# A two-block language model layer on one core: the RWKV inverse kept in both triangular forms, new lengths and grouped pieces in the scheduler, three more slots

## The chip, the core and the metric

The kernel runs on one core of one Trainium2 chip. The metric is the device time of one launch in microseconds (us). Shown are the median of three runs and the profile of one execution.

## What is computed

256 tokens with 1024 features go through two transformer blocks. The first block projects the normed stream into three branches: an RWKV-7 recurrence (8 heads of 64), stick-breaking attention (8 heads of 64), and attention over a memory of 256 rows (4 heads of 128). The branches are gated, merged, projected and added, and a convolutional feed-forward layer follows. The second block has ALiBi attention beside an HGRN-2 recurrence, then a PEER layer (for each token and head 16 of 16384 experts), and a final norm. The part that the change touches most is the recurrence of RWKV-7:

```python
def step(S, inp):
    r_t, w_t, k_t, v_t, kk_t, a_t = inp
    sa = jnp.einsum('bhij,bhj->bhi', S, -kk_t)
    S = (S * w_t[:, :, None, :]
         + sa[..., None] * (kk_t * a_t)[:, :, None, :]
         + v_t[..., None] * k_t[:, :, None, :])
    y_t = jnp.einsum('bhij,bhj->bhi', S, r_t)
    return S, y_t
```

The kernel computes it in chunks of 64 tokens. Within a chunk each head needs the inverse of I + A, where A is strictly lower triangular, 64 x 64; there are 8 heads and 4 chunks, so 32 such inverses.

## The kernel before

**Recording and scheduling.** The kernel's methods don't issue instructions; they record them. Each recorded operation has an engine, a modelled length, and the tiles that it reads and writes. Consecutive products on TensorE that write the same bank are recorded as one piece (`Program.op`, lines 244 to 281) while the piece's modelled length stays under 0.7 us; between two banks that are written in turn this is allowed too where a flag, `join`, is set. `Program.run` (lines 304 to 440) then lays out an order for each engine by list scheduling: of the operations whose inputs are ready by the model and whose tiles have a free slot, the one that can start first, and among those that can start at the same time the one with the longest remaining path. It also models TensorE's clock, and when that is low it prefers operations that fill the array. `emit` (line 442) issues everything from one line, 456, so every instruction of the trace carries L456 (or L450, for table loads); tiles tell the instructions apart. The order on an engine is fixed at build time; on the chip, semaphores between engines decide when each instruction starts.

**The two programs.** Everything up to the PEER layer's start (block 1, block 2, the first PEER queries) is laid out as one program (line 1757), the PEER layer and the final norm as a second one (line 1765, `serial=True`). In the second, operations other than weight products go first on TensorE.

**Weight products.** All large products are computed in three fp32r passes (hi x hi, hi x lo, lo x hi), so each weight tile is loaded by DMA (tile `wraw`), rounded by ScalarE (`whi`) and subtracted by VectorE (`wlo`). Their PSUM banks are tile `psg` (three banks); everything smaller uses tile `ps` (five banks). In one form 256 columns stream per product, in the other 512; `mm` (line 502) models the length.

**Slots.** Working tiles of 1024 words take one of 25 slots (`NSLOT`, line 1782) from their first use to their last. Groups of work (rwkv, stick, mem, gates, main) have reserves of slots and of PSUM banks (line 1784).

**RWKV and its inverse.** `rwkv` starts at line 777. Token-major forms and the Gram matrices (`at`, `bt`, `ct`, `et`) come first, with 64 x 64 products, two chunks side by side in the array. The inverse (lines 927 to 963) is built by doubling, from blocks of 2 to blocks of 64. `tu` holds the upper form (transposed inverse), `tl` the lower one; both are kept for two token blocks (`tb`) of 8 heads and 2 chunks each. At each of four levels `pairs` (line 896) multiplies `at` and `tl`, VectorE masks the result into `y`, `pairs` multiplies `y` and `tu`, VectorE subtracts that from `tu`, and `lower(tb)` (line 931) transposes `tu` into `tl`. A last level has blocks of 32.

```python
        for b in LEVELS[:-1]:
            mb = bcm(self.cst(f"m{b}"), 8)
            for tb in range(2):
                self.mul(y[:, tb], pairs(self.ps(), at, tl, tb), mb)
            for tb in range(2):
                self.sub(tu[:, tb], tu[:, tb], pairs(self.ps(), y, tu, tb))
                lower(tb)
```

[...] 

Behind the inverse come W, the chunk's map G (`g_done`, line 983), the states and the outputs, a group norm, and the split into `yh` and `yl`. The gates' loop then uses the branches in the order stick, memory, RWKV.

Of the kernel before, what the change touches and what calls it, by code (L numbers as in the profile page):

```python
# [19 lines left out]
P = 128  # L20
T = 256
# [65 lines left out]
# ---------------------------------------------------------------------------  # L87
# Tiles and instructions are first recorded; an order of issue is then laid
# out by list scheduling (longest remaining path first) and handed to Tile,
# which places the semaphores.  # L90
# [5 lines left out]
# activation functions outside every table set, the time of a switch  # L96
TABLE = {AF.Exp: "e", AF.Ln: "e", AF.Sigmoid: "s", AF.Tanh: "s", AF.Sqrt: "q", AF.Silu: "w", AF.Gelu: "g"}
SWITCH = 1.28
WINDOW = 3.4133

# [37 lines left out]
class Buf:  # L138
    """A tile: it holds one of its tag's slots from its first use to its last."""
# [68 lines left out]
class Op:  # L208
    __slots__ = ("eng", "calls", "cost", "deps", "succ", "bufs", "first", "level", "ndep", "ready", "idx", "table", "start", "area", "gemm", "bonus", "prio")


class Program:
    def __init__(self, tc):
        self.tc, self.nc = tc, tc.nc
        self.ops, self.tags, self.pools = [], {}, {}
        self.group = None
        self.reserve = {}
        self.count = 0
        self.free_at = {e: 0.0 for e in ("PE", "ACT", "DVE", "POOL", "SP")}
        self.dma_free = 0.0  # L220
        self.bonus = 0.0
        # tiles that the next instruction takes along, to have them before it holds others
        self.also = ()
        self.merge = True
        self.table = None
        self.win, self.work, self.cold = 0.0, 0.0, True
        self.join = False

# [15 lines left out]
    def op(self, eng, method, args, kw, reads, writes, cost, area=1.0, hold=(), gemm=False):  # L244
        call = (eng, method, args, kw)
        last = self.ops[-1] if self.ops else None
        if (eng == "PE" and self.merge and last is not None and last.eng == "PE" and last.cost + cost < 0.7 and last.area == area
# [4 lines left out]
        else:  # L252
            o = Op()
            o.eng, o.calls, o.cost, o.deps, o.bufs, o.idx = eng, [call], cost, {}, {}, len(self.ops)
            o.gemm, o.bonus = gemm, self.bonus
# [27 lines left out]
    # ------------------------------------------------------------ scheduling  # L283
    # the tensor engine's clock is halved for a window of 3.41 us if the array
    # did little work in the window before
# [6 lines left out]
    def clock(self, s, o):  # L292
# [9 lines left out]
        return t - s  # L302

    def run(self, reserve=None, serial=False):
# [53 lines left out]
        while left:  # L358
            best = None
            for e in engines:  # L360
# [3 lines left out]
                if e == "PE":  # L364
                    self.window(f)
                    keep = self.cold or self.work < KEEP * (f - self.win)
                for o in ready[e]:
# [39 lines left out]
            else:  # L407
# [3 lines left out]
                if o.eng == "PE":  # L411
                    end = s + self.clock(s, o)
                free_at[o.eng] = end
            order.append((s, len(order), o))
# [44 lines left out]
class Kernel:  # L459
# [9 lines left out]
    # ---------------------------------------------------------------- helpers  # L469
# [32 lines left out]
    def mm(self, out, lhsT, rhs, start=True, stop=True, skip=False, hold=None, after=None):  # L502
        n = rhs.n
        if rhs.dt == F32:
            cost = max(n / 600, lhsT.shape[1] / 640) + 0.005
        elif rhs.dt == F32R:
            cost = n / 2400 + 0.0025
        else:
            cost = n / 2400 + 0.0025
# [3 lines left out]
        elif area == 0.25:  # L513
            cost = 0.029 + 0.00084 * n
        elif rhs.dt == F32:
            area *= n / 600 / cost
# [3 lines left out]
        self.pr.op("PE", "matmul", (out, lhsT, rhs), kw, [lhsT, rhs, after], [out], cost, area, hold or (), rhs.dt == F32R)  # L520

    # in_ [k, m] -> out [m, k]
    def tr(self, out, in_):
        self.pr.op("PE", "transpose", (out, in_, self.cst("ident")), {}, [in_], [out], 0.11, TR_AREA)

    # the same for 64 x 64 of half rr of the partitions, in place (a transpose's output starts at partition 0)
    def tr64(self, out, in_, rr):
        if rr.start:
            self.mm(out, in_, self.cst("ident")[rr, rr])
            return  # L530
        self.pr.op("PE", "transpose", (out, in_, self.cst("ident")[rr, rr]), {}, [in_], [out], 0.0425, TR_AREA / 4)
# [49 lines left out]
    # after: not before this has been computed  # L581
# [13 lines left out]
    # a weight tile of n columns, loaded at once, as parts of up to 1024 columns  # L595
# [28 lines left out]
    # out^T tiles: [128 features, 256 tokens] in pairs, one PSUM bank per pair;  # L624
    # weight tiles are [128 k, 2 features blocks, kt, 128]
    # early: the first tiles, whose last products wait for the last two k-tiles
# [23 lines left out]
    # natural: [128 tokens, 512 features] for both token blocks; weight tiles are [128 k, 4 kt, 512]  # L650
# [16 lines left out]
    # 1 / sqrt(mean of squares + eps) per token, on every partition  # L667
# [26 lines left out]
    # (x * g) * rstd, split  # L694
# [7 lines left out]
    # x * g, split; the products are to be scaled by rstd, which is returned  # L702
# [7 lines left out]
    # rstd with tokens on partitions  # L710
# [8 lines left out]
    # both features of a bank by rstd  # L719
# [23 lines left out]
    # sums over each head's 64 features of [128 (2 heads), 4, 256] -> [128 t, (tb, 8 heads)]  # L743
# [8 lines left out]
    # [128 t, (tb, 8 heads)] repeated over each head's 64 features  # L752
# [6 lines left out]
    # -> PSUM [128 (2 heads x 64), 256 t] for pair p  # L759
# [4 lines left out]
    # ---------------------------------------------------------------- block 1: RWKV  # L764
# [12 lines left out]
    def rwkv(self, R, K, V, L):  # L777
# [7 lines left out]
        # decay, learning rate  # L785
# [12 lines left out]
        # kk, normalised per head  # L798
# [16 lines left out]
        # k' = k (1 + (a - 1) k_a), b = kk a  # L815
# [4 lines left out]
        # decays within chunks of 64  # L820
# [10 lines left out]
        # kappa = kk P_{t-1}, rho = r P_t, b / P, k' / P; the bonus times v  # L831
        # (kappa and rho side by side, two pairs of heads per tile)
# [10 lines left out]
        # scaled to the chunk's end  # L843
# [10 lines left out]
        # token-major forms: [128 t, (tb, 8 heads, 64)]  # L854
        NB, NE_, NV = self.get("nb"), self.get("ne"), self.get("nv")
        # (kappa and B V side by side, a tile per token block)
# [12 lines left out]
        # Gram matrices per head and chunk, stacked over the two chunks of a token block  # L869
# [22 lines left out]
        # products with v: B V, V^T E^T, and the state's increment from k'  # L892
        YT, H = self.get("yt"), self.get("h")

        # per head and chunk: left^T right, the two chunks of a block side by side in the array
# [11 lines left out]
        # banks by chunk parity u; f(p, tb, u, par, rows of the chunk, out)  # L907
# [19 lines left out]
        # (I + A)^-1 by doubling  # L927
# [3 lines left out]
        def lower(tb):  # L931
            ps = self.ps()
            for h in range(8):
                for rr in half:
                    self.tr64(ps[rr, h * 64:h * 64 + 64], tu[rr, tb, h, :], rr)
            act(tl[:, tb], ps.rearrange("p (h d) -> p h d", h=8))

        for tb in range(2):
            self.mul(tu[:, tb], at[:, tb], bcm(self.cst("m1"), 8))
            self.sub(tu[:, tb], id8, tu[:, tb])  # L940
            lower(tb)
        for b in LEVELS[:-1]:
# [3 lines left out]
            for tb in range(2):  # L946
                self.sub(tu[:, tb], tu[:, tb], pairs(self.ps(), y, tu, tb))
                lower(tb)
        # the last level: one block of 32 below the diagonal
# [19 lines left out]
        # W = -T [kappa | B V]  # L969
# [9 lines left out]
        # per chunk: the state's map G^T, its increment H, and Z in place of rho  # L979
# [3 lines left out]
        def g_done(u, b, ps):  # L983
            g = q422(G)[:, :, b, u, :]
            tb = b.start
            self.mul(g[:, :, 0, :], bcm(self.cst("id2"), 4), peu[:, :, tb, u, :].to_broadcast([P, 4, 64]))
            self.add(g, g, ps)
# [14 lines left out]
        # states S_1 = H_0, S_{c+1} = G_c S_c + H_c, in place of H (slot c holds S_{c+1})  # L1002
# [12 lines left out]
        # outputs y^T  # L1015
# [12 lines left out]
        # group norm per head, gains, bonus, gate  # L1028
# [35 lines left out]
    # ---------------------------------------------------------------- block 1: stick breaking  # L1064
# [5 lines left out]
    # 1 / rms of each head's features, [128 t, (tb, heads)], of [128 t, (tb, 512)]  # L1070
# [13 lines left out]
    # [128 t, (tb, 512)] -> PSUM [128 features, (2 of the blocks, 256 t)], block pair pp  # L1084
# [62 lines left out]
    # ---------------------------------------------------------------- block 1: memory  # L1147
# [44 lines left out]
    # ---------------------------------------------------------------- block 1  # L1192
# [6 lines left out]
    def block1(self):  # L1199
# [12 lines left out]
        pr.group = "stick"  # L1212
        rs = self.rstd_n(rb)
        S = self.big(3, "sb")
        for n, x in enumerate(S):
            self.gemm_n("w_sb", (n * 2, n * 2 + 1), hh, hl, self.evac_n(lambda tb: x[:, tb * 512:(tb + 1) * 512], rs))
        self.stick(*S)
        pr.group = "mem"
        ME = self.big(2, "mem")
        self.load_x(ME, "memT", H[0])  # L1220
        MH = self.big(4, "mh", F32R)
        mh, ml = self.ktiles(MH[:2]), self.ktiles(MH[2:])
        rm = self.norm_late(ME, "mem_norm_g", mh, ml, RE[1])
        MK, MV = self.big(2, "mkv")
        rsm = self.rstd_n(rm)
        for n, x in enumerate((MK, MV)):
            self.gemm_n("w_mem", (n * 2, n * 2 + 1), mh, ml, self.evac_n(lambda tb: x[:, tb * 512:(tb + 1) * 512], rsm))
        pr.group = "mem"
        MQ = self.get("mq")
        self.gemm_n("w_memq", range(2), hh, hl, self.evac_n(lambda tb: MQ[:, tb * 512:(tb + 1) * 512], rs))  # L1230
        self.memory(MQ, MK, MV)
# [636 lines left out]
```

## Time and profile before

| what | value |
| --- | --- |
| device time, median of 3 runs | 1618.37 us (1616.47 to 1623.98) |
| span of the profiled execution | 1608.7 us |
| TensorE (PE) busy | 1569.9 us, 98% |
| VectorE (DVE) busy | 1158.2 us, 72% |
| ScalarE (ACT) busy | 763.9 us, 47% |
| GpSimd (POOL) busy | 124.9 us, 8% |
| mean granted TensorE clock | 0.984 |
| DMA | 249.13 MB, mean 155 GB/s |

The span is counted from the first to the last instruction. Of the profiled execution the page gives the span alone; the runs' median is 9.7 us above it. Engine times are unions of instruction times; matmuls are pipelined and their ends are modelled, so a busy TensorE may still be waiting inside a train of small products. The granted clock is 1.00 at full speed (2.4 GHz) and 0.5 at the lower level (1.2 GHz).

### The profile page before, as it was taken

The numbers are of one execution on the slowest core, as the hardware profiler recorded it, in microseconds if no ns is written. First come the engines' busy times: TensorE is split into PE (matmuls) and PEld (weight loads), VectorE is DVE, ScalarE is ACT, GpSimd is POOL, SyncE is SP. The second block draws the span as 40 slices with busy tenths as digits, with TensorE's granted clock in tenths as the row PEclk, the third lists the DMA queues.
The fourth block names the chain that finished last, engine by engine and source line by source line (L and its number), as shares of the span: only waits on it lengthen the run. The fifth ranks groups of instructions, "written<-read, shape, count | busy, mean of one in ns | idle before, by whom it ended". The sixth has DMA issues, their size and how long they took to land.

```text
span 1608.7 us, 29184 instructions
## 1 busy us (share of the span) xinstructions
PE 1569.9 (98%) x12260; PEld 1422.0 (88%) x12260; DVE 1158.2 (72%) x1970; ACT 763.9 (47%) x1026; POOL 124.9 (8%) x112
## 2 busy tenths in 40 slices
PE   6999999999999999899999999999999999999998
PEld 5976778999999999779999999999998888888886
DVE  8872246666898866977878789888867888555554
ACT  4642246544576645365544445433344333444444
POOL 5010000002321112402000000000000000000000
PEclk9988799999999999999999999999999999999999
DMA  6420122255555545233554455434344444555553
GB/s 220 157 79 27 53 80 80 100 186 187 184 184 184 181 169 223 79 139 125 184 184 174 172 183 184 180 132 158 133 167 172 147 156 157 183 183 189 200 188 131
DMA packets 38436, 249.13 MB, mean 155 GB/s; under 512 B 4000, under 2 KB 7456, under 8 KB 9504
## 3 DMA queue, kind: packets, MB, share of 16 engines
q1 hardware_dynamic: 38304, 247.26, 42.7%
q8 instruction: 96, 1.57, 0.4%
q14 instruction: 36, 0.29, 0.1%
HBM read 246.19 MB, written 1.05 MB: 154 GB/s over the span
## 4 chain that ended last, share of the span: by engine, by line
PE 90%; DVE 6%; ACT 1%; issue 1%; DMA 1%; POOL 0%; SPq 0%; DVEq 0%; ACTq 0%; POOLq 0%
PE psg L456 53%; PE out L456 22%; PE ps L456 10%; PE g L456 4%; DVE wlo L456 2%; DVE hn L456 1%; ACT whi L456 1%; DMA wraw<-in_u 0%; DVE act L456 0%; PE sc L456 0%; DMA wraw<-in_w_rwkv 0%; DVE qt L456 0%; DVE tmp L456 0%; DVE mh L456 0%; ACT act L456 0%
## 5 line engine op out<-in xcount | busy, mean ns | idle before, releaser
L456 DVE TENSOR_TENSOR wlo<-wraw,whi 128x1024 fp32r<-128x1024 f32 (+1 forms) x458 | 572.6, 1255 | 316.3 <-ACT whi L456 314.8
L456 ACT ACTIVATE whi<-wraw 128x1024 fp32r<-128x1024 f32 (+1 forms) x458 | 481.8, 1056 | 651.5 <-PE psg L456 408.3
L456 PE MATMUL psg<-hn,whi 128*128 128x256 f32 x3808 | 692.2, 284 | 12.8 <-ACT whi L456 10.1
L456 PEld LDWEIGHTS psg<-hn,whi 128*128 128x128 f32 x3808 | 591.1, 190 | 14.9 <-ACT whi L456 10.1
L456 PE MATMUL psg<-hn,wlo 128*128 128x256 f32 x1904 | 539.8, 284 | 9.0 <-DVE wlo L456 9.0
L456 PEld LDWEIGHTS psg<-hn,wlo 128*128 128x128 f32 x1904 | 361.7, 190 | 11.0 <-DVE wlo L456 10.9
L456 PE MATMUL out<-whi,hn 128*128 128x512 f32 x1024 | 326.4, 395 | 0.0
L456 PEld LDWEIGHTS out<-whi,hn 128*128 128x128 f32 x1024 | 193.0, 188 | 41.8
L456 PE MATMUL out<-wlo,hn 128*128 128x512 f32 x512 | 200.7, 392 | 0.0
L456 PEld LDWEIGHTS out<-wlo,hn 128*128 128x128 f32 x512 | 96.3, 188 | 20.4
L456 PE MATMUL psg<-whi,hn 128*128 128x512 f32 x224 | 86.2, 428 | 0.3 <-ACT mkv L456 0.2
L456 PE MATMUL g<-ob,oa 128*128 128x64 f16 x1024 | 74.4, 241 | 0.0
L456 PEld LDWEIGHTS <-oa 128*128 128x128 f16 x1024 | 63.1, 118 | 9.7 <-issue 5.9
L456 PEld LDWEIGHTS psg<-whi,hn 128*128 128x128 f32 x224 | 43.2, 193 | 12.7 <-issue 1.8
L456 PE MATMUL psg<-gh,wlo 128*128 128x256 f32 x176 | 49.7, 282 | 0.7 <-DVE wlo L456 0.7
L456 PE MATMUL psg<-gl,whi 128*128 128x256 f32 x176 | 49.5, 281 | 0.0
L456 PE MATMUL psg<-gh,whi 128*128 128x256 f32 x176 | 49.4, 281 | 0.0
L456 DVE TENSOR_TENSOR ob<-ob,ix 128x512 f16<-128x512 f16 x128 | 49.2, 418 | 0.0
L456 PE MATMUL psg<-yl,whi 128*128 128x256 f32 x160 | 45.1, 282 | 0.3 <-DVE yl L456 0.3
L456 PE MATMUL psg<-yh,wlo 128*128 128x256 f32 x160 | 45.1, 282 | 0.2 <-DVE wlo L456 0.2
L456 PE MATMUL psg<-wlo,hn 128*128 128x512 f32 x112 | 45.3, 405 | 0.0
L456 PE MATMUL psg<-yh,whi 128*128 128x256 f32 x160 | 45.1, 282 | 0.0
(317 smaller groups left out, 1813.7 us busy)
## 6 DMA issues: line engine op xcount, KB each, us to landing
wraw<-in_u SPq DMA_DIRECT2D x64, 1024.0 KB, 4.7
wraw<-in_v SPq DMA_DIRECT2D x64, 1024.0 KB, 4.8
wraw<-in_w_up SPq DMA_DIRECT2D x22, 1024.0 KB, 4.8
wraw<-in_w_gate SPq DMA_DIRECT2D x12, 1024.0 KB, 4.8
wraw<-in_w_out SPq DMA_DIRECT2D x8, 1024.0 KB, 4.8
wraw<-in_w_down SPq DMA_DIRECT2D x8, 1024.0 KB, 4.8
wraw<-in_w_q SPq DMA_DIRECT2D x8, 1024.0 KB, 4.8
wraw<-in_w_rwkv SPq DMA_DIRECT2D x6, 1024.0 KB, 4.8
```

What stands on the lines that cost most here:

```text
L456: getattr(eng[e], method)(*[lower(x) for x in args], **{k: lower(x) for k, x in kw.items()})
```

## The change

The inverse keeps both forms up to date. `lower` and `tr64` go. At the start `tl` is made by products of `tu` with the identity; at each level a second product, `pairs(tu, y)`, gives the update of `tl`, which VectorE subtracts. G's diagonal is added with four `scalar_tensor_tensor` in place of a multiplication ahead and an addition behind. In the scheduler, pieces may be up to 1.5 us long; lengths of fp32r, fp16 and 64 x 64 products are changed; each operation knows its array mode (how many rows and columns of the array it uses), a change of mode is modelled as 0.1 us, and in the first program TensorE's next operation is picked among those that can start within 0.11 us of the first one, the longest path first, with a stay of 1.0 us in full-array mode before it is left. There are 28 slots, and the DMA scratch ring is 1024 in place of its default. The three blocks of `block1` (stick, memory's keys and values, memory's queries) become functions, called in the same order as before.

```diff
-        def lower(tb):
+
+        for tb in range(2):
+            self.mul(tu[:, tb], at[:, tb], bcm(self.cst("m1"), 8))
+            self.sub(tu[:, tb], id8, tu[:, tb])
             ps = self.ps()
             for h in range(8):
                 for rr in half:
-                    self.tr64(ps[rr, h * 64:h * 64 + 64], tu[rr, tb, h, :], rr)
+                    self.mm(ps[rr, h * 64:h * 64 + 64], tu[rr, tb, h, :], self.cst("id2")[rr, :])
             act(tl[:, tb], ps.rearrange("p (h d) -> p h d", h=8))
-
-        for tb in range(2):
-            self.mul(tu[:, tb], at[:, tb], bcm(self.cst("m1"), 8))
-            self.sub(tu[:, tb], id8, tu[:, tb])
-            lower(tb)
...
             for tb in range(2):
-                self.sub(tu[:, tb], tu[:, tb], pairs(self.ps(), y, tu, tb))
-                lower(tb)
+                pu = pairs(self.ps(), y, tu, tb)
+                pl = pairs(self.ps(), tu, y, tb)
+                self.sub(tu[:, tb], tu[:, tb], pu)
+                self.sub(tl[:, tb], tl[:, tb], pl)
...
-            g = q422(G)[:, :, b, u, :]
-            tb = b.start
-            self.mul(g[:, :, 0, :], bcm(self.cst("id2"), 4), peu[:, :, tb, u, :].to_broadcast([P, 4, 64]))
-            self.add(g, g, ps)
+            for q in range(4):
+                self.stt(q422(G)[:, q, b.start, u, :], self.cst("id2"), peu[:, q, b.start, u, :], ps[:, q, 0, :],
+                         ALU.mult, ALU.add)
```

```diff
-        if (eng == "PE" and self.merge and last is not None and last.eng == "PE" and last.cost + cost < 0.7 and last.area == area
+        if (eng == "PE" and self.merge and last is not None and last.eng == "PE" and last.cost + cost < (MERGE if mode == (P, P) else MERGE_S) and last.area == area and last.mode == mode
                 and (self.join or {w.buf for w in writes} == {w for w, x in last.bufs.items() if x})):
...
+    def pick(self, ready, f, keep, slot_time):
+        found = []
+        first = None
+        for o in ready:
+            s = max(o.ready, f)
+            if first is not None and s > first + SLACK:
+                continue
+            st = slot_time(o)
+            if st is None:
+                continue
+            s = max(s, st)
+            other = o.mode != self.mode
+            lv = o.prio
+            if keep and o.area > 0.5:
+                lv += 1e6
+            if other:
+                if f - self.since < (BURST if self.mode == (P, P) else BURST_S):
+                    lv -= 1e7
+                s += DRAIN
+            found.append((s, o, lv))
+            first = s if first is None else min(first, s)
...
         elif rhs.dt == F32R:
-            cost = n / 2400 + 0.0025
+            cost = n / 2400 + 0.0125
         else:
-            cost = n / 2400 + 0.0025
+            cost = max(n / 2400 + 0.0025, 0.061)
...
         elif area == 0.25:
-            cost = 0.029 + 0.00084 * n
+            cost = (0.006 + 0.0008 * n) * (0.8 if self.pr.join else 1.0)
...
-NSLOT = 25
+NSLOT = 28
+MERGE = 1.5
+BURST = 1.0
+BURST_S = 0.0
+SLACK = 0.11
+MERGE_S = 1.5
+ORDER1 = "smq"
...
-    nc = _bacc.Bacc("TRN2", target_bir_lowering=False, num_devices=1)
+    nc = _bacc.Bacc("TRN2", target_bir_lowering=False, num_devices=1, dynamic_dma_scratch_size=1024)
```

## Rows read from the trace of the kernel before

**Rows 1.** The page: its first line, busy time by engine (with the share of the span and the number of instructions), and the chain of work that ended last, by engine.

```profile
span 1608.7 us, 29184 instructions
...
PE 1569.9 (98%) x12260; PEld 1422.0 (88%) x12260; DVE 1158.2 (72%) x1970; ACT 763.9 (47%) x1026; POOL 124.9 (8%) x112
...
PE 90%; DVE 6%; ACT 1%; issue 1%; DMA 1%; POOL 0%; SPq 0%; DVEq 0%; ACTq 0%; POOLq 0%
```

**Rows 2.** Busy time by engine in stretches of the span. Columns: the stretch and its length in us; for each engine the busy us and, in brackets, the instructions; the granted TensorE clock (1.00 is full speed); the busy share of the DMA engines; GB/s.

```profile
60.00:300.00 240.00, 238.55 (x2274) 180.10 (x2274) 127.32 (x220) 112.32 (x179) 4.85 (x3) 0.91 0.19 66
...
384.00:428.00 44.00, 40.68 (x329) 39.26 (x328) 33.64 (x34) 21.02 (x32) 21.46 (x16) 1.00 0.47 168
...
566.00:620.00 54.00, 52.57 (x436) 51.91 (x436) 34.07 (x35) 23.61 (x29) 16.92 (x14) 1.00 0.52 184
620.00:800.00 180.00, 170.54 (x1270) 157.29 (x1270) 147.04 (x258) 96.69 (x149) 35.15 (x23) 1.00 0.39 142
800.00:820.00 20.00, 19.14 (x163) 18.94 (x162) 17.23 (x52) 8.05 (x11) 0.00 (x0) 1.00 0.54 204
820.00:1608.00 788.00, 782.29 (x5612) 709.89 (x5610) 580.15 (x1064) 346.59 (x410) 0.00 (x0) 1.00 0.47 168
```

**Rows 3.** The same view in windows of 20 us, for the instructions alone that write or read tile psg (the banks of the weight products). Columns: the window; busy us of TensorE, its weight loads, VectorE and ScalarE; the granted clock; DMA share and GB/s of the whole core.

```profile
100.00:120.00 20.00, 4.50 (x12) 2.29 (x12) 0.00 (x0) 0.68 (x1) 0.80 0.01 2
120.00:140.00 20.00, 7.08 (x19) 3.58 (x19) 0.00 (x0) 0.00 (x0) 0.91 0.15 54
140.00:160.00 20.00, 6.14 (x15) 3.06 (x15) 0.00 (x0) 0.00 (x0) 0.74 0.01 2
160.00:180.00 20.00, 3.58 (x12) 2.02 (x12) 0.00 (x0) 0.00 (x0) 0.74 0.15 53
180.00:200.00 20.00, 7.64 (x19) 4.53 (x20) 0.00 (x0) 1.36 (x2) 0.83 0.15 54
200.00:220.00 20.00, 10.91 (x36) 5.82 (x35) 0.00 (x0) 1.36 (x2) 1.00 0.15 54
220.00:240.00 20.00, 12.08 (x42) 7.43 (x42) 0.00 (x0) 0.00 (x0) 1.00 0.25 86
240.00:260.00 20.00, 12.05 (x39) 6.55 (x39) 0.00 (x0) 1.36 (x2) 1.00 0.21 75
```

**Rows 4.** From the view of tile yl, the subtraction that ends RWKV's output (duration in ns as shortest, median, longest; first and last start in us).

```profile
L456 DVE TENSOR_TENSOR yl<-yt,yh x1: 1212/1212/1212, 285.8 to 285.8; 128x1024 fp32r<-128x1024 f32 x1
```

**Rows 5.** The chain of waits in order of time (start, us, engine, tile, line, xcount): the first long piece behind 300 us.

```profile
300.65 82.03 PE psg L456 x690
```

**Rows 6.** Groups of instructions over the whole span, shapes kept apart: line, engine, operation, out<-in, shapes, xcount | busy us, mean ns of one | idle time before them, and what ended it. All carry line 456, from which every recorded operation is issued.

```profile
L456 PE MATMUL ps<-ci,tu 64*64 64x64 f32 x240 | 40.1, 266 | 1.2 <-DVE tu L456 1.2
...
L456 PE MATMUL ps<-tl,at 64*64 64x64 f32 x256 | 12.9, 264 | 0.0
...
L456 DVE SCALAR_TENSOR_TENSOR tmp<-stk,cv,tmp 128x254 f32<-128x254 f32 x44 | 19.0, 474 | 0.0
...
L456 PE MATMUL ps<-tu,y 64*64 64x64 f32 x256 | 9.4, 221 | 0.0
...
L456 ACT ACTIVATE tl<-ps 128x512 f32<-128x512 f32 x10 | 6.0, 595 | 45.2 <-PE ps L456 45.2
...
L456 DVE TENSOR_TENSOR tu<-tu,ps 128x512 f32<-128x512 f32 x8 | 5.5, 686 | 5.5 <-PE ps L456 5.4
```

**Rows 7.** The timeline of TensorE from 166 us: start, us, engine, line, operation, out<-in, shapes, xcount.

```profile
165.99 3.49 PE L456 MATMUL ps<-ci,tu 64*64 64x64 f32 x24
...
171.00 5.19 PE L456 MATMUL ps<-ci,tu 64*64 64x64 f32 x24
...
176.84 1.97 PE L456 MATMUL ps<-tl,at 64*64 64x64 f32 x32
...
180.02 1.15 PE L456 MATMUL ps<-tl,at 64*64 64x64 f32 x32
```

**Rows 8.** The chain of waits in order of time: start, us, engine, tile, line, xcount. Of TensorE's pieces of three on psg between 97 and 260 us the first and the last (there are 39), and of the pieces between them four.

```profile
102.24 1.58 PE psg L456 x3
...
238.20 0.39 PE ps L456 x16
238.59 0.89 PE psg L456 x3
...
245.01 0.62 PE ps L456 x32
...
251.80 1.58 PE psg L456 x6
...
259.28 0.70 PE psg L456 x3
```

**Rows 9.** The same chain, where VectorE writes tile g.

```profile
93.29 1.71 DVE g L456
...
239.93 0.42 DVE g L456
```

**Rows 10.** The page's DMA queues: kind, packets, MB, share of 16 engines' time.

```profile
q1 hardware_dynamic: 38304, 247.26, 42.7%
q8 instruction: 96, 1.57, 0.4%
q14 instruction: 36, 0.29, 0.1%
```

More of the change, by code (lines that the diff above doesn't have):

```diff
@@ L99 @@
 WINDOW = 3.4133
+DRAIN = 0.1
 def _split_pattern(side):
@@ L208 @@
 class Op:
-    __slots__ = ("eng", "calls", "cost", "deps", "succ", "bufs", "first", "level", "ndep", "ready", "idx", "table", "start", "area", "gemm", "bonus", "prio")
+    __slots__ = ("eng", "calls", "cost", "deps", "succ", "bufs", "first", "level", "ndep", "ready", "idx", "table", "start", "area", "gemm", "bonus", "prio", "mode", "end")
 class Program:
@@ L227, in __init__ @@
         self.join = False
+        self.mode, self.since = (P, P), 0.0
     def tag(self, name, pool, slots, fifo=False):
@@ L242, in buf, with op @@
         return View(b, arr, [], dt)
-    def op(self, eng, method, args, kw, reads, writes, cost, area=1.0, hold=(), gemm=False):
+    def op(self, eng, method, args, kw, reads, writes, cost, area=1.0, hold=(), gemm=False, mode=(P, P)):
         call = (eng, method, args, kw)
         last = self.ops[-1] if self.ops else None
-        if (eng == "PE" and self.merge and last is not None and last.eng == "PE" and last.cost + cost < 0.7 and last.area == area
+        if (eng == "PE" and self.merge and last is not None and last.eng == "PE" and last.cost + cost < (MERGE if mode == (P, P) else MERGE_S) and last.area == area and last.mode == mode
                 and (self.join or {w.buf for w in writes} == {w for w, x in last.bufs.items() if x})):
@@ L254, in op @@
             o.eng, o.calls, o.cost, o.deps, o.bufs, o.idx = eng, [call], cost, {}, {}, len(self.ops)
-            o.gemm, o.bonus = gemm, self.bonus
+            o.gemm, o.bonus, o.mode = gemm, self.bonus, mode
             o.succ, o.first, o.table, o.area, o.start = [], [], None, area, None
@@ L302, in clock @@
         return t - s
+    def pick(self, ready, f, keep, slot_time):
[19 more added lines that the diff above has]
+            first = s if first is None else min(first, s)
+        if not found:
+            return None
+        best = max((x for x in found if x[0] <= first + SLACK), key=lambda x: (x[2], -x[0]))
+        return (max(best[1].ready, f, slot_time(best[1])), best[1], best[2])
     def run(self, reserve=None, serial=False):
@@ L366, in run @@
                     keep = self.cold or self.work < KEEP * (f - self.win)
+                    if not serial:
+                        cand = self.pick(ready[e], f, keep, slot_time)
+                        if cand is not None and (best is None or cand[0] < best[0]):
+                            best = cand
+                        continue
                 for o in ready[e]:
@@ L411, in run @@
                 if o.eng == "PE":
+                    if o.mode != self.mode:
+                        self.mode, self.since = o.mode, s
+                        end += DRAIN
+                        s += DRAIN
                     end = s + self.clock(s, o)
                 free_at[o.eng] = end
+            o.end = end
             order.append((s, len(order), o))
@@ L519, in mm @@
             kw["skip_group_check"] = True
-        self.pr.op("PE", "matmul", (out, lhsT, rhs), kw, [lhsT, rhs, after], [out], cost, area, hold or (), rhs.dt == F32R)
+        mode = tuple(32 if n <= 32 else 64 if n <= 64 else 128 for n in lhsT.shape)
+        self.pr.op("PE", "matmul", (out, lhsT, rhs), kw, [lhsT, rhs, after], [out], cost, area, hold or (), rhs.dt == F32R, mode)
     def tr(self, out, in_):
         self.pr.op("PE", "transpose", (out, in_, self.cst("ident")), {}, [in_], [out], 0.11, TR_AREA)
[L527 to L531, printed above, removed]
     def act(self, out, in_, func=AF.Copy, bias=None, scale=None, accum_out=None):
@@ L1211, in block1, with sticks, mems, memq @@
         self.rwkv(R, K, V, L)
-        pr.group = "stick"
         rs = self.rstd_n(rb)
[L1214 to L1231, printed above, removed]
+        done = {}
+        def sticks():
+            pr.group = "stick"
+            S = self.big(3, "sb")
+            for n, x in enumerate(S):
+                self.gemm_n("w_sb", (n * 2, n * 2 + 1), hh, hl,
+                            self.evac_n(lambda tb: x[:, tb * 512:(tb + 1) * 512], rs))
+            self.stick(*S)
+        def mems():
+            pr.group = "mem"
+            ME = self.big(2, "mem")
+            self.load_x(ME, "memT", H[0])
+            MH = self.big(4, "mh", F32R)
+            mh, ml = self.ktiles(MH[:2]), self.ktiles(MH[2:])
+            rm = self.norm_late(ME, "mem_norm_g", mh, ml, RE[1])
+            MK, MV = done["kv"] = self.big(2, "mkv")
+            rsm = self.rstd_n(rm)
+            for n, x in enumerate((MK, MV)):
+                self.gemm_n("w_mem", (n * 2, n * 2 + 1), mh, ml,
+                            self.evac_n(lambda tb: x[:, tb * 512:(tb + 1) * 512], rsm))
+        def memq():
+            pr.group = "mem"
+            MQ = self.get("mq")
+            self.gemm_n("w_memq", range(2), hh, hl, self.evac_n(lambda tb: MQ[:, tb * 512:(tb + 1) * 512], rs))
+            self.memory(MQ, *done["kv"])
+        for o in ORDER1:
+            {"s": sticks, "m": mems, "q": memq}[o]()
         pr.group = "gates"
```

## The prediction

> **What bounds the kernel now.** I read the page first: its chain of what ended last is 90% TensorE, and TensorE is busy for 1569.9 of 1608.7 us [rows 1]. The table of stretches says where the other 39 us are: 1.4 us idle in the 240 us from 60 to 300, 3.3 around 384 to 428, 1.4 in 566 to 620, 9.5 in 620 to 800, 0.9 in 800 to 820, 5.7 in the 788 us behind [rows 2], and some 16 elsewhere, by subtraction. So hardly any time can be won by removing waits; it has to come out of what TensorE does. Behind 820 us it does large products without a gap and nothing of the diff changes them. The stretch from 60 to 300 is different: the products of the weights (tile psg) are a small part of it. From 100 to 200 us they fill 4.50 + 7.08 + 6.14 + 3.58 + 7.64 = 28.9 us of 100, and in just these windows the granted clock is 0.74 to 0.91; from 200 us on they fill 10.9 to 12.1 of 20 and the clock is 1.00 [rows 3]. The rest of TensorE's time there goes to small tiles: RWKV's 64x64 work and two attentions.
>
> **Who is late there?** RWKV's last split ends at 287 us [rows 4], and its output is wanted only by the last of three branches, in the unbroken run of gate products that starts at 300.65 [rows 5]. From 300 us on there are 82 us of products, most of which need no RWKV. RWKV's chain of waits therefore has tens of microseconds to spare: it may get longer or shorter without moving the end. What moves it is TensorE's total work. That is why I add TensorE time and not latencies.
>
> **1. The inverse without transposes.** Before, each update of tu is followed by lower(): 8 transposes and 8 products with the identity, alternating between the two halves of the array, 24 instructions in the trace. There are 10 such sets. The grouped rows give 240 instructions 40.1 us, while 256 instructions of products of the same 64x64x64 size take 12.9 us (tl,at) and 9.4 us (tu,y) [rows 6]. The timeline agrees: one set of 24 lasts 3.49 us, or 5.19 where the clock was low, and a set of 32 products lasts 1.15 or 1.97 [rows 7]. The transposes' spacing, 3.49/24 = 0.145 us an instruction, is four times that of the products, 1.15/32 = 0.036.
> Afterwards 2 of the 10 sets are products of tu with id2 (16 products, 32 instructions each) and 8 are pairs(tu, y), of exactly the tu,y form. Removed: 40.1. Added: 10 sets x 32 = 320 instructions, at 9.4/256 or 12.9/256 us each 11.8 to 16.1 us. Net **-24 to -28**, I take -26.
> The Trainium skill speaks against this part: "TensorE: Matmul & The Clock Gate", Terms, has a transpose mode that is 4 times faster for FP32. By that, going over to products would cost and not save; it is priced as a rival below. The row decides: the sets with transposes are the slow ones.
> Eight copies of tl by ScalarE (595 ns) go and eight subtractions by VectorE (686 ns) come [rows 6], 5.5 us on VectorE. They lie beside TensorE's other work; if that cover failed, up to 0.7 us a level and token block would stand on RWKV's chain only, which has room. Both products of a level now hold a PSUM bank at once: a token block takes two of the five small banks where it took one. That can delay the next small piece, not the weight products, which have three banks of their own. Cost zero, bound 0 to 3.
>
> **2. Grouped pieces.** Weight products are recorded in pieces up to 0.7 us: three of 512 columns. Between small tiles a piece of three takes 0.89 us, a piece of six 1.58: the second three cost 0.69, so 0.20 is paid for entering and leaving. On the small side 16 instructions take 0.39 and 32 take 0.62, so 0.16 is fixed there [rows 8]. From 97 to 260 us the chain has 39 pieces of three, the first at 102.24, the last at 259.28 [rows 8]. With 1.5 us and the longer cost, six fit (6 x 0.226 = 1.36): some 20 pairs of changes go, 20 x 0.36 = 7. Small pieces grow too (all 16 products of a pairs() in one, where it was eight). I take **-8**; bounds 0 (the 39 are not next to each other in the new order) and -15.
>
> **3. Clock.** The five windows from 100 to 200 us lose 20 x (0.20 + 0.09 + 0.26 + 0.26 + 0.17) = 19.6 us of full-speed time [rows 3]. About 5 of it is inside the transposes' 40.1 (10 x 3.49 = 34.9) and already counted; 14 are left. With the transposes gone, the same 28.9 us of weight products lie in about 72 us, 8 in 20, between the window with 7.64 (clock 0.83) and that with 10.91 (1.00). An estimate of 0.88 from these two leaves 0.12 x 72 = 8.6 lost: **-6**; bounds 0 and -14.
>
> **4. G's diagonal.** The multiplication by the identity that stands on the chain at 93.29 us (1.71) goes [rows 9]. TensorE was idle for 1.2 us behind it, so at most -1.2. At the end four scalar_tensor_tensor of 128x64 replace one 0.42 us addition [rows 9]; the nearest row is 0.474 us for 254 columns [rows 6], so each is below that, the four below 1.9, twice, beside other products. Zero; bounds -1 and +1.
>
> **5. Slots, scheduler lengths, ring.** The page's DMA traffic has one hardware queue and two of instruction loading [rows 10], so the ring that shrinks carries nothing: zero. Three more slots let gates' and attention's tiles start earlier; TensorE is idle for 1.4 us from 60 to 300, so there is nothing there for them to fill: zero. The new lengths and the pick of an operation within 0.11 us re-lay the order everywhere in the first part. That can win or lose at its borders, where TensorE was idle for 15 us after 300 in all [rows 2]. Those borders are norms and scans, in which VectorE leads (busy for 147 of the 180 us from 620 to 800 [rows 2]), and it gets no less work there. Zero, bounds -10 and +10. In the part behind 820 us the gate products keep their piece of 16 and the value products their piece of three, since each piece ends at its bank; idle there is 5.7 us. Zero.
>
> **Sum.** -26 - 8 - 6 = -40 us, on a profiled span of 1608.7. The median of the runs is 1618.4, 9.7 above the span; I let that stand: **1578 us**. The outer ends: 24 - 3 - 1 - 10 = 10 us won, 28 + 15 + 14 + 1 + 10 = 68 won; all ends together are unlikely, so the forecast's own range is 1556 to 1602.
>
> **Rivals.**
> *A. The clock recovers wholly.* If the slow instructions alone kept it down, the 14 us all come back: -26 - 8 - 14 = -48, 1570. For it: the longest low stretches hold sets of transposes (5.19 us for one set). Against: other small work is in the same windows. The Trainium skill ("TensorE: Matmul & The Clock Gate", Part 4) says that transposes do not count as activity for the clock; that would favour this case, and no row here separates it from the plain low share of large products. Chance 0.12.
> *B. Pieces don't group.* The 39 pieces of three stay apart because the new order still puts a small piece behind each: -26 - 6 = -32, 1586. Chance 0.08.
> *C. The time is given back.* VectorE and ScalarE feed the weight products (split by ScalarE, then VectorE). If the shortened stretch makes them late, TensorE waits where it was filled. Both were far from full there, VectorE busy for 127 and ScalarE for 112 of 240 us [rows 2], which speaks against it. It would leave 0 to 15 us, 1610. Chance 0.08.
> *D. Slower: the clock falls.* Larger small pieces mean longer runs without a large product. Each us at half clock costs 0.5 us of TensorE work. To eat the 34 us of parts 1 and 2 the stretch must be at half speed for 68 us more than the present 39 (19.6 x 2); all 160 us to 260 at half would be 121 more, -34 + 60 = +26, 1644; half way to the worst, 95 more, about +14, 1632. Against: windows with 10.9 us of large products in 20 ran at full clock although small tiles filled the rest. Chance 0.06.
> *E. Transposes are the cheap form.* If a transpose cost a quarter of a product, the added 320 instructions would cost what they do now and the removed ones 3 to 4 us: +10 instead of -26, sum -4, 1614. The 40.1 us row contradicts it. Chance 0.01. (It is the Terms rule of that page of the Trainium skill, carried over to this kernel.)
>
> **How the numbers follow.** Forecast 0.65, A 0.12, B 0.08, C 0.08, D 0.06, E 0.01. Forecast, A and B are faster; about 0.5% (8 us) is what a measurement can tell from no change. C is half on each side of 1610. So faster 0.65 + 0.12 + 0.08 less a tail of 0.02, plus half of C: 0.87; same: the other half of C, E and that tail, 0.07; slower D, 0.06. The range takes in forecast, A and B, from 1553 (A with part of the other ends) to 1604, and leaves out C, D and E, 0.15, and tails.
>
> **What would show it.** In the profile after: no ci,tu group of 40 us, products of tu and y in 512 instructions, with the new form, that take 19 to 26 us in all, up to 1.15 us a set of 32; weight pieces of six at 1.58 us between small tiles; granted clock at 0.85 or more in the windows where the inverse lies; the unbroken run of gate products starting at about 260 instead of 300.65; the part behind the PEER boundary as long as now, 788 us. Wrong: if the gates' run starts 40 us earlier and the end doesn't, if the new products are slower than 1.2 us a set, or if the clock row shows 5 for whole slices.

## The result and the profile after

The changed kernel takes **1559.66 us** (median of 4 runs, 1558.85 to 1563.08) against 1617.45 for the kernel before in the same session: 0.9646 of it, 95% interval [0.9616, 0.9676], 57.8 us less. The forecast was 1578 us, 40 us less. All medians in this text are of runs in the chip's fast state: one slow run, of the inverse alone (5881 us), is left out.

The page of the profile after, the lines that answer to [rows 1]:

```profile
span 1557.1 us, 29335 instructions
...
PE 1519.8 (98%) x12340; PEld 1398.3 (90%) x12340; DVE 1160.4 (75%) x1982; ACT 764.1 (49%) x1021; POOL 126.6 (8%) x112
...
PEclk9999999999999999999999999999999999999999
```

TensorE still sets the time, with 50 us less to do. The last line is the granted clock in 40 slices of 39 us; nowhere is a slice below 0.9. The chain of waits after (start, us, what) shows the new pattern and the landmarks, as [rows 5, 8] did before:

```profile
110.34 1.59 PE psg L497 x6
111.94 3.97 PE ps L497 x104
...
117.30 2.01 PE ps L497 x64
119.31 1.59 PE psg L497 x6
120.90 2.01 PE ps L497 x64
122.92 1.57 PE psg L497 x6
...
245.73 85.58 PE psg L497 x720
...
768.81 22.74 PE psg L497 x192
```

and of before, the landmark that [rows 5] lacks, PEER's first long run:

```profile
819.91 22.73 PE psg L456 x192
```

Six weight products alternate with 64 instructions of small tiles, where it was three with 16 to 32. The gates' run starts at 245.73 instead of 300.65, PEER's at 768.81 instead of 819.91. So:

| stretch | before, us | after, us | difference |
| --- | --- | --- | --- |
| 60 us to the gates' run | 240.7 | 185.7 | -54.9 |
| to PEER's run | 519.3 | 523.1 | +3.8 |
| to the end of the span | 788.8 | 788.3 | -0.5 |

That is 51.6 us of span. The other 6 lie in the median of before, see the ring below. The instructions that read or write psg alone, with the granted clock as the column behind ScalarE's busy time, as in [rows 3]:

```profile
100.00:120.00 20.00, 5.88 (x22) 3.82 (x22) 0.00 (x0) 0.68 (x1) 1.00 0.24 87
120.00:140.00 20.00, 9.18 (x34) 5.62 (x33) 0.00 (x0) 0.69 (x1) 1.00 0.16 55
140.00:160.00 20.00, 10.00 (x36) 6.29 (x36) 0.00 (x0) 1.10 (x2) 1.00 0.16 55
160.00:180.00 20.00, 9.97 (x36) 6.29 (x36) 0.00 (x0) 0.26 (x1) 1.00 0.31 107
180.00:200.00 20.00, 7.66 (x30) 5.38 (x31) 0.00 (x0) 1.37 (x2) 1.00 0.16 54
```

The clock is full in all of them, also with 5.88 us of 20. The groups that take the place of the transposes, as in [rows 6]:

```profile
L497 PE MATMUL ps<-y,tu 64*64 64x64 f32 x256 | 8.5, 220 | 0.3 <-DVE y L497 0.3
...
L497 PE MATMUL ps<-ce,tu 64*64 64x64 f32 x64 | 2.3, 221 | 0.1
...
L497 PE MATMUL ps<-tu,y 64*64 64x64 f32 x256 | 8.7, 220 | 0.0
```

The first two, 8.5 + 2.3 = 10.8 us, replace 40.1. The third was there before, with 9.4.

### The profile page after: what moved, and what is told of

Same layout as the page of the kernel before. It is cut to its first block, busy times and chain, and to the rows that moved or that the text cites. A ratio compares the mean times of both kernels' runs of the same rounds, so it can differ in the third digit from the quotient of the medians.

```text
span 1557.1 us, 29335 instructions
## 1 busy us (share of the span) xinstructions
PE 1519.8 (98%) x12340; PEld 1398.3 (90%) x12340; DVE 1160.4 (75%) x1982; ACT 764.1 (49%) x1021; POOL 126.6 (8%) x112
## 3 DMA queue, kind: packets, MB, share of 16 engines
q8 instruction: 96, 1.57, 0.4%
## 4 chain that ended last, share of the span: by engine, by line
PE 86%; DVE 8%; ACT 2%; issue 2%; DMA 1%; POOL 1%; POOLq 0%; SPq 0%; ACTq 0%; DVEq 0%
PE psg L497 52%; PE out L497 23%; PE ps L497 6%; PE g L497 4%; DVE wlo L497 3%; DVE hn L497 1%; ACT whi L497 1%; POOL sq L497 0%; PE sc L497 0%; DVE mh L497 0%; DMA wraw<-in_w_recqf 0%; DVE qt L497 0%; DVE small L497 0%; DVE rkv L497 0%; ACT mo L497 0%
## 5 line engine op out<-in xcount | busy, mean ns | idle before, releaser
L497 DVE TENSOR_TENSOR wlo<-wraw,whi 128x1024 fp32r<-128x1024 f32 (+1 forms) x458 | 563.1, 1233 | 280.8 <-ACT whi L497 276.9
L497 PE MATMUL psg<-whi,hn 128*128 128x512 f32 x224 | 76.9, 405 | 0.3 <-ACT rg L497 0.3
L497 DVE TENSOR_TENSOR oa<-ix,iof 128x1024 f16<-128x1024 f16 x64 | 44.2, 690 | 6.3 <-PE g L497 6.1
```

The source lines that it names most:

```text
L497: getattr(eng[e], method)(*[lower(x) for x in args], **{k: lower(x) for k, x in kw.items()})
```

## The experiments

All ratios are to the kernel before on the same chip, with a 95% interval in brackets; "us less" compares with its median there, which lay between 1616.47 and 1618.63. The kernel after (1559.66) was not run again beside the experiments, so a difference from it of a microsecond or two says nothing. My theory was that TensorE's time adds up: inverse, then clock, then grouping.

**1. Each half of the change alone.** The new inverse in the kernel before (the inverse's lines of the diff and nothing else), and the kernel after with the old inverse:

```diff
-                self.sub(tu[:, tb], tu[:, tb], pairs(self.ps(), y, tu, tb))
-                lower(tb)
+                pu = pairs(self.ps(), y, tu, tb)
+                pl = pairs(self.ps(), tu, y, tb)
+                self.sub(tu[:, tb], tu[:, tb], pu)
+                self.sub(tl[:, tb], tl[:, tb], pl)
```

> The kernel before with the new inverse alone (no transposes, tl updated by a second product), old scheduler, 25 slots. Theory 1 (TensorE time adds up, the transposes were the largest term and also kept the clock low): the 40 us of ci,tu become 10 to 13, and the granted clock rises to 1.00 in the windows of the inverse: 38 to 46 us less than before, 1572 to 1580. Rival (the clock recovers only through the grouped pieces): the clock stays at 0.8 to 0.9 where the inverse lies, 26 to 32 us less, 1586 to 1592. Rival (the gain is the scheduler's): under 15 us less.

> The kernel after with the old inverse (transposes) put back; scheduler, pieces, slots, G and ring as after. Theory 1: only the grouping of pieces and a part of the clock remain, 10 to 22 us less than before, 1596 to 1607, and 36 to 48 us above the kernel after. Rival (the gain is the scheduler's): 30 us or more below before, within 25 of after. Rival (the transposes, now in unbroken groups, fill a longer stretch at half clock): as slow as before or slower.

Measured: inverse alone 1581.72 us, 0.9791 [0.9751, 0.9832], 35 us less, between theory 1's range (38 to 46) and the first rival's (26 to 32); the rest alone 1594.43, 0.9894 [0.9849, 0.9938], 22 less, the upper end of theory 1's range. Together 57 of 58: the halves add up, as far as the second's four runs (1588.75 to 1604.08) can tell. The first run is not purely a gain of TensorE time. Its windows (all instructions: TensorE, its loads, VectorE, ScalarE, GpSimd, clock, DMA share, GB/s) show TensorE idle for 7 and 6 us of 20, no DMA, and a low clock: from 140 to 160 us no weight product runs, and TensorE waits for VectorE's and ScalarE's steps on tile stk. My forecast gave TensorE other work at all times.

```profile
140.00:160.00 20.00, 12.99 (x73) 10.63 (x72) 10.67 (x25) 10.56 (x22) 0.00 (x0) 0.82 0.00 0
150.00:170.00 20.00, 14.31 (x81) 11.87 (x80) 10.34 (x23) 8.44 (x18) 0.00 (x0) 0.76 0.00 1
```

(The windows overlap by 10 us.) Eight of the inverse's ten sets come behind this, from 174.6 us on, and there the clock is 1.00, as theory 1 had it.

**2. The ring alone**, in the kernel before.

```diff
-    nc = _bacc.Bacc("TRN2", target_bir_lowering=False, num_devices=1)
+    nc = _bacc.Bacc("TRN2", target_bir_lowering=False, num_devices=1, dynamic_dma_scratch_size=1024)
```

> The kernel before with the DMA scratch ring at 1024 and nothing else. The runs stood 8.8 us above the profiled span before and 2.6 us after. Theory 1 (the ring carries nothing): no difference, 1615 to 1620, span 1608.7 within 2. Rival (the ring costs time outside the span): 4 to 8 us less, 1609 to 1613, with the span as before.

Measured: 1617.51 us, 1.002 [0.9997, 1.0043]. No effect. But its profile, of the same instructions in the same order as before, has a span 6 us longer, and in six of the windows of [rows 3] a clock that is different:

```profile
100.00:120.00 20.00, 20.00 (x222) 14.92 (x221) 8.59 (x13) 8.23 (x14) 0.00 (x0) 0.84 0.01 2
120.00:140.00 20.00, 20.00 (x133) 12.86 (x129) 2.60 (x3) 3.01 (x5) 0.00 (x0) 0.68 0.15 54
140.00:160.00 20.00, 20.00 (x181) 13.82 (x180) 4.50 (x8) 6.12 (x9) 0.00 (x0) 0.76 0.01 2
160.00:180.00 20.00, 20.00 (x171) 14.05 (x171) 6.47 (x11) 3.73 (x6) 0.00 (x0) 0.76 0.15 53
180.00:200.00 20.00, 20.00 (x191) 14.99 (x190) 6.47 (x10) 4.97 (x8) 0.00 (x0) 0.70 0.00 1
200.00:220.00 20.00, 20.00 (x253) 13.95 (x251) 7.68 (x14) 6.54 (x10) 0.00 (x0) 0.83 0.31 107
```

Full-speed time lost here is 20 x (0.16 + 0.32 + 0.24 + 0.24 + 0.30 + 0.17) = 28.6 us, against 19.6 in the profile of before: 9 more, of which 6 show in the span. 23 runs of before beside this lay between 1608.23 and 1621.80. The profile of before (span 1608.7) caught an execution at the lower end; here 1.8 us lie around the span (1616.47 on 1614.7), after 1.75 (1558.85 on 1557.1). So of the "9.7 us around the span" some 8 were no fixed cost, and the clock is what differs between the two profiles.

**3. What makes the transposes slow.** lower() made of products, and lower() with its loops turned round, both in the kernel before (`tr64` issues a transpose for the first half of the partitions, a product with the identity for the second):

```diff
-                    self.tr64(ps[rr, h * 64:h * 64 + 64], tu[rr, tb, h, :], rr)
+                    self.mm(ps[rr, h * 64:h * 64 + 64], tu[rr, tb, h, :], self.cst("id2")[rr, :])
```

> The kernel before with lower() made of 16 products with the identity, no transposes; tl still comes from tu through a bank and a ScalarE copy. Theory 1 (the transposes' TensorE time is what counts, not the length of the chain): a set of 32 takes 0.8 to 1.2 us where 24 took 3.5, and the time is within 8 us of the run with the new inverse alone (1582): 1576 to 1592. Rival (the shorter chain of the two forms is what counts): 1600 or more.

```diff
-            for h in range(8):
-                for rr in half:
+            for rr in half:
+                for h in range(8):
                     self.tr64(ps[rr, h * 64:h * 64 + 64], tu[rr, tb, h, :], rr)
```

> The kernel before with lower()'s loops turned round: first the 8 transposes of one half of the array, then the 8 products of the other. Theory 1 (a change between transposing and multiplying is what costs 0.145 us an instruction): the sets fall from 40 us to under 20 in all, 12 to 25 us less than before, 1592 to 1605. Rival (every transpose is slow by itself): the 8 transposes stay at 0.2 us or more each, the 16 instructions of the products take the usual 0.6: 5 to 15 us less. Rival (waiting on one half of the array): no change, 1612 to 1620.

Measured: products 1588.12 us, 0.982 [0.9782, 0.9859]; loops turned 1573.87, 0.9735 [0.9697, 0.9772], **43 us less from the order of two loops**, three quarters of the whole change and more than any of the theories had put on it; the products came out as theory 1 expected. The same 8 transposes and 8 products, one kind behind the other (timeline of TensorE: start, us; first the transposes, then the products, then what follows):

```profile
117.79 0.63 PE L456 MATMUL ps<-ci,tu 64*64 64x64 f32 x8
...
118.35 1.14 PE L456 MATMUL ps<-ci,tu 64*64 64x64 f32 x16
...
119.42 0.70 PE L456 MATMUL ps<-turned,turned 64*128 64x256 f32 x2
```

and of before, what follows the set that starts at 165.99 in [rows 7]:

```profile
169.42 1.22 PE L456 MATMUL ps<-stk,ce 128*128 128x128 f32 x4
```

From the starts, 8 transposes take 0.56 us and the 8 products, two instructions each, 1.07, so 1.63 for a set that took 169.42 - 165.99 = 3.43 before. What cost was the change between the two kinds, fifteen of them a set, some 0.12 us each ((3.43 - 1.63) / 15). It isn't the change between the halves of the array: with products alone the sets change halves just as often, and ten of them, of 32 instructions each, take 11.7 us. With alternation in the kernel after (the rest alone, at nearly full clock) ten sets take 32.9:

```profile
L456 PE MATMUL ps<-ce,tu 64*64 64x64 f32 x320 | 11.7, 221 | 1.2 <-DVE tu L456 1.2
...
L497 PE MATMUL ps<-ci,tu 64*64 64x64 f32 x240 | 32.9, 240 | 0.1
```

A change of kind within one half was not run. And the clock of the run with turned loops:

```profile
100.00:120.00 20.00, 20.00 (x258) 15.74 (x258) 11.69 (x18) 9.66 (x16) 0.00 (x0) 0.87 0.01 2
120.00:140.00 20.00, 20.00 (x296) 15.26 (x295) 7.58 (x14) 7.09 (x12) 0.00 (x0) 1.00 0.16 54
140.00:160.00 20.00, 20.00 (x304) 15.90 (x304) 8.15 (x13) 4.69 (x8) 0.00 (x0) 1.00 0.15 54
160.00:180.00 20.00, 20.00 (x370) 15.51 (x368) 7.75 (x16) 7.39 (x13) 0.00 (x0) 1.00 0.16 54
```

It is full from 120 us on, with the limit on a piece still 0.7 us. But the edit changes more than the order within a set. A transpose and a product have different areas in the scheduler's model and never join into a piece, so a set was 16 pieces of one call and is two pieces now, and the order around the sets is laid out anew. So it isn't shown that the alternation by itself kept the clock down, and two windows of 4 us of before show that it doesn't always: the set that starts at 97.25 us ran into half clock, and the one from 108.41 on, also alternating, with three weight products in its middle, ran at full clock.

```profile
100.00:104.00 4.00, 4.00 (x16) 2.79 (x17) 1.45 (x4) 0.70 (x2) 0.00 (x0) 0.50 0.00 0
...
108.00:112.00 4.00, 4.00 (x26) 2.59 (x25) 2.40 (x4) 0.94 (x2) 0.00 (x0) 1.00 0.00 0
```

The turned loops are also 8 us faster than the new inverse alone (1581.72), the run in which TensorE was left without work.

The kernel after with this turned old inverse asks whether two forms are needed at all:

> The kernel after with the old inverse, but with lower()'s loops turned round (8 transposes, then 8 products). Theory (the alternation was the cost, the second form is only a little cheaper on TensorE): transposes' sets 17 us where the new form has 10.4, so 5 to 12 us above after, 1564 to 1572. Rival (the shorter chain of the two forms matters): 20 us or more above after, 1580 or more. Rival (fewer products, no second subtraction): at or below after.

Measured: 1566.63 us, 0.968 [0.9656, 0.9704], 7 above after, as the theory had it, and 28 below the same kernel with the loops not turned (the rest alone, 1594.43): the second pair of runs that differ in these two loops alone. Its ten sets take 16.3 us where the new form has 10.8, so 5.5 of the 7 are TensorE's time:

```profile
L497 PE MATMUL ps<-ci,tu 64*64 64x64 f32 x240 | 16.3, 219 | 0.1
```

**4. Pieces.** The kernel after with short pieces, first `MERGE = MERGE_S = 0.7`, then 0.73:

> The kernel after with pieces of at most 0.7 us of either kind again (three products of 512 columns); inverse, lengths, pick and slots as after. Theory 1: the changes of mode come back, 6 to 12 us above after, 1566 to 1572, clock still 1.00. Rival (grouping holds the clock up): the clock falls below 0.9 in two or more of the windows from 100 to 180 us, 15 to 25 us above after. Rival (the pick groups them in any case): within 3 us of after, weight products still six at a time.

> The kernel after with pieces of at most 0.73 us: three products of 512 columns or six of 256, as in the kernel before (0.7 us with the new lengths gave five of 256, which cuts through the groups of three). Theory 1 (grouping is worth 8 to 15 us between small tiles, and the rest of the 51 us came from pieces of five): 1566 to 1580, weight products outside the RWKV stretch as fast as after. Rival (the pick needs long pieces everywhere, else it mixes two banks): 1595 or more, with waits of ScalarE's rounding for TensorE in the feed-forward stretch.

Measured: 1611.44 us, 0.9968 [0.995, 0.9987], nearly all of the gain gone, and 1579.18, 0.9766 [0.9722, 0.981]. None of my expectations held for the first. Its clock stays up (0.91 from 100 to 120 us, then 1.00). The gates' run begins at 260.54, 15 us after that of the kernel after; PEER's at 819.56, so a further 36 are lost in the large products between. The chain of waits in the feed-forward layer there:

```profile
445.56 10.58 PE psg L497 x87
...
456.17 1.01 DVE stk L497 x2
...
457.37 1.22 DVE wlo L497
...
458.64 1.44 PE psg L497 x10
```

and at 0.73 us, where this chain has no wait:

```profile
419.93 33.12 PE psg L497 x275
```

Every 13 us TensorE waits for VectorE, which first empties a bank (stk) and then makes the next weights (wlo). With the new length (0.119 us) 0.7 us hold five products of 256 columns, which cuts through the three passes of a k-tile; at 0.73 there are six, and 32 us come back, to the upper end of what theory 1 expected there. That five out of step cause the waits is shown by this pair; by which order of the two banks it does so I haven't followed. The 19.5 us still above after are what long pieces are worth in this scheduler; in the old one the same step is 14 (1581.72 with the inverse alone, 1567.64 with inverse and pieces, in 5).

**5. Which parts of the scheduler.** Without the pick; old choice and lengths with new inverse and pieces of 1.5 us; longer pieces; 25 slots:

> The kernel after without the pick among operations that start within 0.11 us and without the stay in full-array mode (the first program chooses as before: earliest start, longest path among equals); long pieces, lengths and slots as after. Theory (long pieces do the grouping, the pick adds little): within 8 us of after, 1556 to 1568. Rival (the pick is what groups): pieces again change mode as often as before, 1572 to 1590.

> The kernel before with the new inverse and with pieces up to 1.5 us, nothing else (old lengths, old choice, 25 slots). Theory (inverse and long pieces are the change): 1556 to 1570. Rival (lengths and pick are needed, else TensorE is fed worse and the clock falls as in the run with the inverse alone): 1572 to 1585.

> The kernel after with weight pieces up to 3.0 us (twelve products of 512 columns, or 24 of 256); small pieces as after. If changes of mode still cost: some 10 pairs fewer at 0.36 us, 3 to 5 us less than after, 1554 to 1557. Rival (longer pieces make the small chains wait and the borders grow): 3 to 15 us more than after.

> The kernel after with 25 slots in place of 28. Theory 1 (slots hold nothing back): within 4 us of after, 1556 to 1564. Rival (the slots feed the stretch): 8 us or more above after.

Measured: no pick 1561.30 us, 0.9645 [0.9624, 0.9666], the same as after; inverse and pieces alone 1567.64, 0.9687 [0.9666, 0.9707], 51 us less than before (both as the theory had it); pieces of 3.0 us 1560.21, 0.9643 [0.9621, 0.9665], the same, which neither expectation had: longer pieces save nothing more; 25 slots 1566.20, 0.9695 [0.9658, 0.9733], 6.5 above after by the medians (span 4.1 longer), between the two expectations and with intervals that overlap: a small effect of the slots is likely, not shown. The 8 us between inverse and pieces alone and the kernel after belong to slots, lengths, pick and G's diagonal together; lengths and G's diagonal were not run by themselves.

## Why the prediction was right, and where not

The mechanism is as forecast, the size less so: 1559.66 us lie 18 below the forecast of 1578, 4 above the lower end of its range, and nearer to rival A's 1570, which had a chance of 0.12.

**What bounds it:** right. TensorE's busy time fell by 50 us and the span by 52; the part behind PEER's start kept its 788 us. That there is always other work for TensorE was too strong: with the inverse alone there wasn't.

**Inverse (-26):** by the rows -29.3 (40.1 to 10.8), so sized rightly; some 7 of it are low clock, as the same alternating sets take 32.9 at nearly full clock. The 512 instructions of tu and y take 8.5 + 8.7 = 17.2 us, just under the 19 to 26 that were to show it. The reason was wrong in part: I read 0.145 us an instruction as the price of transposing. It was the price of alternating, as the turned loops show. Rival E's rule, that a transpose is the cheap form (the Trainium skill, "TensorE: Matmul & The Clock Gate", Terms), points the right way once the kinds are kept apart: 0.56 us for 8 against 1.07 for 8 products here, a half and not a quarter. The products still win, since 16 of them in both halves take 1.08 us (10.8 / 10), no more than the 8 in one half.

**Clock (-6): the term that was mis-sized.** Rival A's clock is what happened. The profile of before lost 19.6 us, about 15 of them outside the transposes, and all came back; and the median of before stood some 6 further above the span than that of after, which I had taken for a constant and which the ring's experiment puts down to clock. With 15 and 6 where I had 6, this is some 15 us of the 18 by which I was short; inverse and grouping add 3 each, and the borders take 4 back. My estimate rested on the share of large products in a window, and that share did not decide it: after, 5.88 us of 20 go with 1.00, before, 7.64 went with 0.83. (It was also read too high: on a straight line between the two windows, 8.0 gives 0.85 and not 0.88, and the term would have been -4.) Of the reason that I named for A, the Trainium skill's sentence (same page, Part 4) that transposes do not count as activity, no run here decides: the run with turned loops has just as many transposes at full clock from 120 us on, but these fill only some 6 us in all (10 x 0.56). What held the clock down stays open; what the runs show is 1.00 from 120 to 200 us in each run whose sets do not alternate and whose TensorE is not left idle there.

**Grouping (-8):** by subtraction 54.9 - 29.3 - 14.6 = 11 in the stretch. The mechanism is as forecast: pieces of six at 1.57 to 1.59 us. The experiments put it higher, 14 us in the old scheduler and 19.5 in the new one, in the whole kernel.

**G, slots, ring, lengths, pick (0):** ring and pick measured as nothing; slots perhaps 4 to 6; G's diagonal and the lengths were not run alone. The borders cost 3.8 us, within the bound of 10.

## What to carry to other kernels

Read the spacing of small TensorE instructions by kind and by order before replacing them: issuing all transposes and then all products gave 43 of the 58 us here, without new arithmetic. Where the clock is low in just the stretch of a slow pattern, price the case that all of the lost clock comes back, in the median of the runs and not only in the one profiled: here it did. A limit on the length of issue groups should fit whole accumulation steps: 0.70 and 0.73 us lay 32 us apart here.

## What was not expected of the hardware

A change between a transpose and an fp32 product in 64x64 tiles of alternating halves costs some 0.12 us, almost twice what either instruction takes by itself (0.07 us from the starts above). Low clock lay where these alternating sets are (before, the ring alone; 0.91 from 140 to 180 us in the rest alone), but also without any transpose where TensorE was idle (0.76 to 0.82 with the inverse alone), and around the first set with the loops turned (0.87 from 100 to 120 us). Executions of one and the same order of instructions differed by 13.6 us (1608.23 to 1621.80); two profiles of it differ in granted clock where the alternation lies. The other kernels with alternating sets spread as far, the ring alone over 12.1 us and the rest alone over 15.3; no other kernel spread over more than 7.6, and most of those were run only four times.
